# GpSimd's operations on two wide tensors move to VectorE, all but those of the input projection

## The chip, the cores and the metric

The kernel runs on one core of a Trainium2 chip. The metric is device time in microseconds (us), the median of three runs; lower is better. The core has TensorE (PE, matrix multiplication into PSUM), VectorE (DVE), ScalarE (ACT), GpSimd (POOL) and SyncE (SP, which here issues most DMAs). Each engine takes its instructions strictly in the order of its own queue and waits on semaphores for the others. GpSimd does not read PSUM in this kernel.

## The reference

A two-layer decoder trunk on x of 1024 tokens by 1024 channels, in float32. Layer 0 mixes with an HGRN2 recurrence and a Conformer convolution behind one input projection, and one output projection follows. Layer 1 mixes with causal pooling over windows of 2, 4, 8 and 16 tokens. Each layer then attends over 256 memory tokens with four heads and applies a SwiGLU FFN of width 2816. Around each sub-layer: x = LayerNorm(alpha * x + f(x)).

```
y = hybrid_ab_mixer(x, ...)  or  multiscale_pool_mixer(x, ...)
x = layer_norm(ALPHA * x + y, ln_mix_g[l], ln_mix_b[l])
y = memory_cross_attention(x, mem_n, xa_wq[l], xa_wk[l], xa_wv[l], xa_wo[l])
x = layer_norm(ALPHA * x + y, ln_xa_g[l], ln_xa_b[l])
y = swiglu_ffn(x, ffn_wg[l], ffn_wu[l], ffn_wd[l])
x = layer_norm(ALPHA * x + y, ln_ffn_g[l], ln_ffn_b[l])
```

## The kernel before, in words

Every float32 product is made of three matmuls (`mm3`, L208): each operand is split into a high part, a copy rounded to the reduced type by ScalarE, and a low part, the difference, by VectorE or GpSimd (`split`, L214; for weights `split_next`, L112, where `lo_engine` names the engine of the low part, lines L123 and L125). TensorE multiplies low by high, high by low and high by high, and cannot begin on an operand before its low part is there.

Larger products use seven block products in place of eight (Strassen's scheme in Winograd's form). `seven` (L807) runs them: for each product j of an order such as (1, 2, 5, 6, 3, 7, 4), for each half g of the inner dimension, it calls `hook(j, g)`, makes operands ahead (`look`, three or four in hand), and lets TensorE run 24 matmuls over four token blocks p. When a product is through, `add(j, p, bank)` adds each of its four PSUM banks into the result, on VectorE (`add_res`, L247) or by ScalarE copies. Products 1, 6, 7 and 4 accumulate on the same four banks, so that the additions of one must be done before the next writes; products 5 and 3 share another four, and product 2 has its own. There are eight banks. `combos_A` and `combos_B` (L725 to L765) make the sums and differences of blocks that the scheme wants, in steps 0 to 3, two operations of 128x1024 each; the hooks call them. `operands7` (L795) splits the A side's operand with GpSimd and the B side's with VectorE. A product of this kind appears as the output projection (`mixer0_out`), the attention scores (`attn_scores`) and the attention output (`attn_out`), the last two in both layers; each has 14 operands. `build_A` and `build_VWo` make the B sides by ordinary matmuls ahead of them and already issue the first combinations and operands.

The FFN's gate and up products use the same scheme with VectorE alone. The down product (`ffn_down`, L1337) runs 42 operands whose A sides come ready from DRAM; its hooks apply the gain and shift of the preceding norm to eight tiles of x (`AFFINE`, L52; L1371 and L1372), on VectorE or GpSimd.

There is no scheduler: an engine's queue is the order in which the code issues. So an addition that TensorE waits for stands behind everything that the hooks and the operand making have issued to VectorE before it. GpSimd also does the one-column steps of the norms (`ln_a`, L257 and L258; `ln_n`, L268; `rstd`, L228), scales seven of eight softmax tiles of each layer (L939, one operation with a broadcast; the other tile takes four one-head instructions on VectorE, L942), and makes the weights' low parts wherever `lo_engine` says so: in the input projection, in the output projection and the value projection behind it, in the attention output, and from the down product to the next build.

Of the kernel before, what the change touches and what calls it, by code (L numbers as in the profile page):

```python
# [12 lines left out]
ALU = mybir.AluOpType  # L13
AX = mybir.AxisListType

P = 128
# [7 lines left out]
MEM = 256  # L24
HEADS = 4
# [25 lines left out]

AFFINE = {(1, 2): ((0, "vector"), (4, "gpsimd")), (1, 3): ((1, "vector"),), (1, 4): ((2, "vector"), (5, "gpsimd")),  # L52
          (1, 5): ((3, "vector"),), (5, 1): ((6, "gpsimd"),), (5, 3): ((7, "vector"),)}

# [90 lines left out]
class Kern:  # L145
# [442 lines left out]
    def mixer0_out(self):  # L588
        nc = self.nc
        gb = self.ln_params(self.a["ln_mix_g"][0], self.a["ln_mix_b"][0])  # L590
        x = self.x = [None] * NT
        sts = [self.sm("lst", 5) for _ in range(NT)]
        A, B = self.sides
        take2 = lambda: [self.w.take() for _ in range(2)]
        Y = lambda i, k: [self.Y[i, k, g] for g in range(2)]

        def load(t):
            x[t] = self.page("x", [D])
            nc.sync.dma_start(x[t], self.a["x"][t * P:(t + 1) * P, :])

        def add(j, p, b):
            self.add_block(j, b, x[p], x[p + 4], sts[p], sts[p + 4])
            if j == 3:
                self.ln_a(x[p], sts[p])
            if j == 4:
                self.w.ahead(4 + (p + 1) // 2, 7)
                self.ln_a(x[p + 4], sts[p + 4])
                if p > 1:
                    self.ln_b(x[p + 2], sts[p + 2], gb)

        def hook(j, g):
            if j == 1:
                if g == 0:
                    while self.y_ready[2] < 4:
                        self.pump()
                    A[2] = Y(0, 1)
                load(2 * g)
                load(2 * g + 1)
                B[("12", 3)[g]] = take2()
                if g == 1:  # L620
                    self.combos_B(B, 0, nc.vector)
                    self.combos_B(B, 1, nc.gpsimd)
            if j == 2 and g == 0:
                while self.bg or self.bg2:
                    self.pump()
                A["blocks"] = ((A[1], A[2]), (Y(1, 0), Y(1, 1)))
                for i in range(3):
                    self.combos_A(A, i, nc.vector)
                self.combos_B(B, 2, nc.gpsimd)
            if (j, g) in ((2, 1), (5, 0)):  # L630
                load(4 + 2 * (j == 5))
                load(5 + 2 * (j == 5))
            if j == 6 and g == 0:
                self.combos_B(B, 3, nc.vector)
                self.combos_A(A, 3, nc.gpsimd)
            if j == 7:
                self.ln_b(x[2 * g], sts[2 * g], gb)
                self.ln_b(x[2 * g + 1], sts[2 * g + 1], gb)
            if j in (7, 4):
                self.w.ahead(1 + g + 2 * (j == 4), 6)  # L640

        self.w.lo_engine = ("gpsimd",)
        self.w.split_ahead = 0
        self.seven(ORDER_A, self.made, self.src, 2, 4, lambda j: 4 if j in (3, 7) else 3, add, hook, 0)
        self.w.split_ahead = 2
        self.last = [lambda t=t: self.ln_b(x[t], sts[t], gb) for t in (6, 7)]
# [77 lines left out]

    def combos_A(self, A, step, eng):  # L725

        tt = eng.tensor_tensor
        if step == 0:
# [18 lines left out]

    def combos_B(self, B, step, eng):
        tt = eng.tensor_tensor
        if step == 0:  # L750
# [43 lines left out]

    def operands7(self, order, fa, fb, ng, fast=()):  # L795

        for j in order:
            for g in range(ng):
                r = []
                for f, eng in ((fa, "vector" if (j, g) in fast else "gpsimd"), (fb, "vector")):  # L800
                    src = f(j, g)
                    hi, lo = self.page("dh", list(src.shape[1:]), F32R), self.page("dl", list(src.shape[1:]), F32R)
                    self.split(hi, lo, src, eng)
                    r += [hi, lo]
                yield r
# [76 lines left out]
    def build_A(self):  # L882
# [6 lines left out]
        for dc in range(DC):  # L889
# [20 lines left out]
            if dc == 3:  # L910
                A["blocks"] = self.AT
                self.combos_A(A, 0, nc.gpsimd)
            if dc in (4, 5):
# [3 lines left out]
            if dc == 5:  # L917
                self.combos_A(A, 1, nc.gpsimd)
            if dc == 6:
                self.combos_A(A, 2, nc.gpsimd)  # L920
                self.combos_B(B, 0, nc.vector)
        self.combos_B(B, 1, nc.vector)
        self.combos_B(B, 2, nc.vector)
        self.sides = A, B
        self.AT, self.x = [None, None], None

    def softmax(self, p, pool):

# [8 lines left out]
        nc.vector.reciprocal(rs, sm)  # L937
        if pool:
            nc.gpsimd.tensor_tensor(p, p, rs.unsqueeze(2).broadcast_to([P, HEADS, MEM]), op=ALU.mult)  # L939
            return  # L940
        for h in range(HEADS):
            nc.vector.tensor_scalar(p[:, h, :], p[:, h, :], rs[:, h:h + 1], None, op0=ALU.mult)  # L942

    def softmaxes(self, ts):

        live = []
        todo = [self.softmax(self.Pm[t], t in (1, 2, 3, 4, 5, 6, 7)) for t in ts]
        while todo or live:
# [7 lines left out]
    def attn_scores(self):  # L956
# [18 lines left out]
        def hook(j, g):  # L975
            if j == 6 and g == 0:
                self.combos_B(B, 3, nc.vector)
                self.combos_A(A, 3, nc.gpsimd)
            if j in (7, 4):
# [8 lines left out]
    def build_VWo(self):  # L988
# [43 lines left out]
        self.made.append(next(self.src))  # L1032
        self.combos_B(B, 0, nc.vector)
        f = self.blocks_T(view[4:])
        A["blocks"] = ((A[1], A[2]), (f[:2], f[2:]))
        self.combos_B(B, 1, nc.vector)
        self.sides = A, B

    def attn_out(self, layer):
# [3 lines left out]
        sts = [self.sm("lst", 6) for _ in range(NT)]  # L1043
        self.w.lo_engine = ("gpsimd",)

# [12 lines left out]
        def hook(j, g):  # L1058
            if j == 1:
                if g == 0:  # L1060
                    self.combos_A(A, 0, nc.gpsimd)
                else:
                    self.combos_A(A, 1, nc.vector)
                    self.combos_A(A, 2, nc.gpsimd)
            if j == 2 and g == 0:
                self.combos_B(B, 2, nc.vector)
            if (j, g) in ((2, 1), (5, 0)):
# [3 lines left out]
            if j == 6 and g == 0:  # L1071
                self.combos_B(B, 3, nc.vector)
                self.combos_A(A, 3, nc.gpsimd)
            if j in (7, 4):
# [262 lines left out]
    def ffn_down(self, layer):  # L1337
        nc = self.nc
        self.w.split_ahead = 0
        self.w.lo_engine = ("gpsimd",)  # L1340
        x = self.x = [None] * NT
# [19 lines left out]
        def hook(j, g):  # L1361
# [5 lines left out]
            if j == 1 and g == 0:  # L1367
                gx.extend(self.ln_params(self.a["ln_xa_g"][layer], self.a["ln_xa_b"][layer]))
            for t, eng in AFFINE.get((j, g), ()):
                eng = getattr(nc, eng)  # L1370
                eng.tensor_tensor(x[t], x[t], gx[0], op=ALU.mult)  # L1371
                eng.tensor_tensor(x[t], x[t], gx[1], op=ALU.add)  # L1372
            if j == 4 and g == 0:
# [250 lines left out]
```

## Time and profile before

| | |
|---|---|
| median of 3 runs | 2451.51 us (2450.9 to 2452.84) |
| profiled execution | 2451.65 us, span 2449.9 us |
| granted TensorE clock | 0.976 of full speed |
| busy, share of the span | PE 94%, PEld 78%, DVE 73%, ACT 43%, POOL 27% |

The busy share of PE is the union of pipelined matmuls, so 94% says that the array has work queued, not that it runs at its peak. A wait is listed as engine, line and what ended it. The stages, by the names of PSUM tiles in the trace: input projection and recurrence to 395 us; output projection 395 to 503; value projection of the memory to 535; build of the scores' B side to 559; scores to 650; build of the output's B side to 681; attention output to 767; FFN gate and up to 1209, down to 1428; then the second layer in the same order, with the key and value projections and the pooling mixer from 1428 to 1537.

### The profile page before, as it was taken

To read this page: it belongs to the slowest core of one execution; us is meant where nothing else is said; L and a number is where in the kernel's file an instruction comes from. 1 tells how busy PE (TensorE), PEld (TensorE's weight loads), DVE (VectorE), ACT (ScalarE), POOL (GpSimd) and SP (SyncE) were. 2 spreads that over 40 slices of the span, in tenths; PEclk is the share of its full clock that TensorE was granted. 3 is DMA by queue.
4 is the path that set the end of the run, shared out by engine and by line. 5 is a ranking of instruction groups with operands and counts; after the bars stand their busy time and mean duration, and the time that the engine had idled before them with its cause. 6 is when DMAs were issued, how large, how long until landed. Compare 5 with 4: busy or idle time off the path is not lost. (4 is left out here: it accounts for less than half of the span.)

```text
span 2449.9 us, 29443 instructions
## 1 busy us (share of the span) xinstructions
PE 2312.4 (94%) x11208; PEld 1916.5 (78%) x11208; DVE 1778.0 (73%) x2126; ACT 1044.2 (43%) x1727; POOL 665.9 (27%) x401
## 2 busy tenths in 40 slices
PE   8999997797979999999999989798999999999998
PEld 7777776696868888888878789786788888887886
DVE  6986788868795876766774566978767667676555
ACT  3245555344736544444412234546364444342212
POOL 1332346757483000000110073755610000002001
PEclk9999999899989999999999999999999999999999
DMA  5111124050122234435796642302024353449783
GB/s 185 69 35 35 35 90 160 26 187 28 53 77 87 95 130 163 159 125 184 280 356 230 247 142 102 118 1 103 36 85 158 126 182 130 161 176 392 261 291 117
DMA packets 117341, 344.02 MB, mean 140 GB/s; under 512 B 10832, under 2 KB 11344, under 8 KB 117200
## 3 DMA queue, kind: packets, MB, share of 16 engines
q1 hardware_dynamic: 70560, 244.35, 27.7%
q10 hardware_dynamic: 46640, 97.79, 11.1%
q8 instruction: 89, 1.46, 0.2%
q14 instruction: 52, 0.43, 0.1%
HBM read 239.34 MB, written 102.76 MB: 140 GB/s over the span
## 5 line engine op out<-in xcount | busy, mean ns | idle before, releaser
L210 PE MATMUL P<-xh,op 128*128 128x512 f32 x1120 | 436.2, 389 | 2.1 <-ACT u L1301 2.1
L212 PE MATMUL P<-xh,op 128*128 128x512 f32 x1120 | 435.7, 389 | 0.0
L211 PE MATMUL P<-xl,op 128*128 128x512 f32 x1120 | 435.7, 389 | 0.0
L210 PE MATMUL D<-dh,dl 128*128 128x512 f32 x560 | 226.2, 404 | 58.4 <-DVE x L247 35.4
L1371 POOL TENSOR_TENSOR x<-x,lng 128x1024 f32<-128x1024 f32 x6 | 17.9, 2980 | 867.8 <-DVE s L1179 421.4
L210 PE MATMUL D<-dh,wp 128*128 128x512 f32 x616 | 242.4, 394 | 9.5 <-ACT dh L215 8.3
L210 PEld LDWEIGHTS P<-xh,op 128*128 128x128 f32 x1120 | 210.2, 188 | 47.3 <-ACT u L1301 3.8
L211 PE MATMUL D<-dl,wp 128*128 128x512 f32 x616 | 243.0, 395 | 3.3 <-DVE dl L216 3.3
L1113 DVE TENSOR_TENSOR op<-raw,op 128x512 fp32r<-128x512 f32 x200 | 137.9, 689 | 147.5 <-ACT op L1112 147.5
L212 PEld LDWEIGHTS P<-xh,op 128*128 128x128 f32 x1120 | 210.2, 188 | 44.0
L211 PE MATMUL D<-dl,dh 128*128 128x512 f32 x560 | 224.6, 401 | 21.1 <-DVE dl L216 21.1
L211 PEld LDWEIGHTS P<-xl,op 128*128 128x128 f32 x1120 | 210.2, 188 | 43.3
L212 PE MATMUL D<-dh,wp 128*128 128x512 f32 x616 | 241.8, 393 | 0.0
L212 PE MATMUL D<-dh,dh 128*128 128x512 f32 x560 | 223.4, 399 | 0.0
L125 POOL TENSOR_TENSOR wl<-raw,wh 128x1024 fp32r<-128x1024 f32 x64 | 173.5, 2723 | 164.3 <-ACT wh L123 159.9
L216 DVE TENSOR_TENSOR dl<-wp,dh 128x1024 fp32r<-128x1024 f32 x96 | 127.6, 1336 | 115.9 <-ACT dh L215 72.8
L215 ACT CAST dh<-wp 128x1024 fp32r<-128x1024 f32 x96 | 93.8, 989 | 265.4 <-DVE wp L777 57.3
L365 DVE SCALAR_TENSOR_TENSOR cacc<-sig,par,cacc 128x1023 f32<-128x1023 f32 (+14 forms) x120 | 175.5, 1462 | 2.5
L210 PEld LDWEIGHTS D<-dh,dl 128*128 128x128 f32 x560 | 108.8, 194 | 85.5 <-issue 36.6
L257 POOL TENSOR_SCALAR lst<-lst 128x1 f32<-128x1 f32 x48 | 27.3, 568 | 466.7 <-ACT sq L256 466.3
L216 POOL TENSOR_TENSOR dl<-xf,dh 128x1024 fp32r<-128x1024 f32 x48 | 141.5, 2965 | 39.6 <-ACT dh L215 29.2
L216 DVE TENSOR_TENSOR dl<-B,dh 128x1024 fp32r<-128x1024 f32 x48 | 117.9, 2488 | 40.7 <-ACT dh L215 40.7
(272 smaller groups left out, 5236.6 us busy)
## 6 DMA issues: line engine op xcount, KB each, us to landing
wp<-hD SPq DMA_DIRECT2D x140, 512.0 KB, 5.8
hD<-sh ACTq DMA_DIRECT2D x66, 512.0 KB, 3.8
raw<-in_wg SPq DMA_DIRECT2D x44, 512.0 KB, 4.2
raw<-in_wu SPq DMA_DIRECT2D x44, 512.0 KB, 3.3
hD<-hf ACTq DMA_DIRECT2D x44, 512.0 KB, 3.7
hD<-s ACTq DMA_DIRECT2D x44, 512.0 KB, 4.6
wp<-in_wd SPq DMA_DIRECT2D x40, 512.0 KB, 7.8
xD<-x ACTq DMA_DIRECT2D x32, 512.0 KB, 3.8
```

What stands on the lines that cost most here:

```text
L125: eng.tensor_tensor(lo, raw, hi.bitcast(F32), op=ALU.subtract)
L210: mm(out, ll, rh, start=start, stop=False, skip_group_check=more)
L211: mm(out, lh, rl, start=False, stop=False, skip_group_check=more)
L212: mm(out, lh, rh, start=False, stop=stop, skip_group_check=more)
L215: self.nc.scalar.copy(hi, src)
L216: getattr(self.nc, lo_engine).tensor_tensor(lo, src, hi.bitcast(F32), op=ALU.subtract)
L257: nc.gpsimd.tensor_scalar(st[:, 3:4], st[:, 3:4], 1.0 / D, LN_EPS, op0=ALU.mult, op1=ALU.add)
L365: nc.vector.scalar_tensor_tensor(acc[:, s:], u[:, :S - s], w[:, j:j + 1], acc[:, s:], op0=ALU.mult, op1=ALU.add)
L1113: getattr(nc, lo_engine).tensor_tensor(pg[:, 1], src, pg[:, 0].bitcast(F32), op=ALU.subtract)
L1371: eng.tensor_tensor(x[t], x[t], gx[0], op=ALU.mult)
```

## The change

Every wide operation that GpSimd had after the input projection is issued to VectorE at the same place in the code: the A side's low parts in `operands7`, all `combos_A` and `combos_B`, the low parts of weights where `lo_engine` was GpSimd, the affine steps, and the softmax scaling, which becomes four instructions for each tile. GpSimd keeps the one-column steps and the low weight parts of the input projection. The computed values are the same.

```diff
-AFFINE = {(1, 2): ((0, "vector"), (4, "gpsimd")), (1, 3): ((1, "vector"),), (1, 4): ((2, "vector"), (5, "gpsimd")),
-          (1, 5): ((3, "vector"),), (5, 1): ((6, "gpsimd"),), (5, 3): ((7, "vector"),)}
+AFFINE = {(1, 2): (0, 4), (1, 3): (1,), (1, 4): (2, 5), (1, 5): (3,), (5, 1): (6,), (5, 3): (7,)}
@@ mixer0_out, attn_out, ffn_down @@
-        self.w.lo_engine = ("gpsimd",)
+        self.w.lo_engine = ("vector",)
...
-    def combos_A(self, A, step, eng):
-
-        tt = eng.tensor_tensor
+    def combos_A(self, A, step):
+
+        tt = self.nc.vector.tensor_tensor
...
-    def combos_B(self, B, step, eng):
-        tt = eng.tensor_tensor
+    def combos_B(self, B, step):
+        tt = self.nc.vector.tensor_tensor
...
-    def operands7(self, order, fa, fb, ng, fast=()):
-
+    def operands7(self, order, fa, fb, ng):
...
-                for f, eng in ((fa, "vector" if (j, g) in fast else "gpsimd"), (fb, "vector")):
+                for f in (fa, fb):
...
-                    self.split(hi, lo, src, eng)
+                    self.split(hi, lo, src)
@@ build_A, and the other callers alike @@
-                self.combos_A(A, 0, nc.gpsimd)
+                self.combos_A(A, 0)
@@ softmax @@
-        if pool:
-            nc.gpsimd.tensor_tensor(p, p, rs.unsqueeze(2).broadcast_to([P, HEADS, MEM]), op=ALU.mult)
-            return
         for h in range(HEADS):
             nc.vector.tensor_scalar(p[:, h, :], p[:, h, :], rs[:, h:h + 1], None, op0=ALU.mult)
@@ ffn_down, hook @@
-            for t, eng in AFFINE.get((j, g), ()):
-                eng = getattr(nc, eng)
-                eng.tensor_tensor(x[t], x[t], gx[0], op=ALU.mult)
-                eng.tensor_tensor(x[t], x[t], gx[1], op=ALU.add)
+            for t in AFFINE.get((j, g), ()):
+                for r, op in zip(gx, (ALU.mult, ALU.add)):
+                    nc.vector.tensor_tensor(x[t], x[t], r, op=op)
```

## Rows read from the trace of the kernel before

**Rows 1.** The page's first part: busy us (share of span) and instructions of each engine.
```profile
PE 2312.4 (94%) x11208; PEld 1916.5 (78%) x11208; DVE 1778.0 (73%) x2126; ACT 1044.2 (43%) x1727; POOL 665.9 (27%) x401
```
**Rows 2.** Waits of TensorE: engine, line, releaser, us in total, times, longest.
```profile
PE D L210 <- DVE x L247: 35.4, 6, 14.8
PE D L211 <- DVE dl L216: 24.4, 7, 10.6
PE D L210 <- POOL dl L216: 23.0, 5, 9.6
...
PE pa L210 <- POOL wl L125: 1.7, 1, 1.7
```
**Rows 3.** Timeline of TensorE: start, us, instruction, [idle before <- what ended it].
```profile
432.93 0.77 PE L210 MATMUL D<-dh,dl 128*128 128x512 f32 x1 [14.79 <-DVE x L247]
...
490.76 0.77 PE L210 MATMUL D<-dh,dl 128*128 128x512 f32 x1 [12.53 <-DVE x L247]
...
583.11 0.80 PE L211 MATMUL D<-dl,dh 128*128 128x512 f32 x1 [10.55 <-DVE dl L216]
...
706.98 0.80 PE L210 MATMUL D<-dh,dl 128*128 128x512 f32 x1 [9.59 <-POOL dl L216]
...
718.71 0.47 PE L210 MATMUL D<-dh,dl 128*128 128x512 f32 x1 [3.38 <-DVE x L247]
...
1243.00 0.80 PE L210 MATMUL D<-dh,wp 128*128 128x512 f32 x1 [4.14 <-ACT dh L215]
...
1440.79 0.58 PE L210 MATMUL pk<-wh,wl 128*128 128x256 f32 x1 [5.67 <-POOL wl L125]
```
**Rows 4.** Windows: length, busy us and instructions by engine, granted clock, DMA share, GB/s.
```profile
394.70:503.50 108.80, 80.62 (x340) 65.30 (x339) 92.40 (x85) 40.32 (x53) 78.97 (x37) 0.87 0.18 65
...
650.00:680.80 30.80, 29.32 (x160) 24.55 (x159) 26.25 (x32) 27.49 (x66) 15.64 (x8) 1.00 0.41 152
...
767.30:1208.80 441.50, 440.41 (x1973) 364.66 (x1972) 312.28 (x448) 206.07 (x327) 7.98 (x14) 1.00 0.43 152
```
**Rows 5.** Timelines of GpSimd and VectorE: wide operations beside each other and alone.
```profile
479.06 9.88 POOL L125 TENSOR_TENSOR wl<-raw,wh 128x1024 fp32r<-128x1024 f32 x3
...
468.25 1.28 DVE L262 SCALAR_TENSOR_TENSOR x<-x,lst,lng 128x1024 f32<-128x1024 f32 x1
...
476.78 3.39 DVE L262 SCALAR_TENSOR_TENSOR x<-x,lst,lng 128x1024 f32<-128x1024 f32 x1
...
581.84 3.48 DVE L216 TENSOR_TENSOR dl<-B,dh 128x1024 fp32r<-128x1024 f32 x3
```
**Rows 6.** Timeline of VectorE ahead of the first stall of the output projection.
```profile
407.62 2.47 DVE L247 SCALAR_TENSOR_TENSOR x<-x,D 128x512 f32<-128x512 f32 x4
410.01 6.72 DVE L732 TENSOR_TENSOR S<-y,y 128x1024 f32<-128x1024 f32 x2
...
432.10 0.68 DVE L247 SCALAR_TENSOR_TENSOR x<-x,D 128x512 f32<-128x512 f32 x1
```
**Rows 7.** Timeline of VectorE in the build ahead of the scores.
```profile
549.40 0.69 DVE L905 COPY B<-pa 128x512 f32<-128x512 f32 x1 [1.05 <-PE pa L212]
```
**Rows 8.** Timeline of VectorE around the start of the attention output.
```profile
659.53 1.22 DVE L125 TENSOR_TENSOR wl<-raw,wh 128x1024 fp32r<-128x1024 f32 x1
...
688.02 2.47 DVE L865 COPY xf<-xt 128x512 f32<-128x512 f32 x4
...
717.88 0.67 DVE L247 SCALAR_TENSOR_TENSOR x<-x,D 128x512 f32<-128x512 f32 x1
```
**Rows 9.** Groups by line and form: softmax scaling on VectorE; busy us, mean ns, idle before.
```profile
L942 DVE TENSOR_SCALAR p<-p,rs 128x256 f32<-128x256 f32 x8 | 2.3, 349 | 0.1
```
**Rows 10.** Timeline of VectorE in the down product.
```profile
1240.13 1.41 DVE L777 TENSOR_TENSOR wp<-wp,wp 128x1024 f32<-128x1024 f32 x1 [4.36 <-DMA wp<-in_wd]
...
1248.89 1.23 DVE L216 TENSOR_TENSOR dl<-wp,dh 128x1024 fp32r<-128x1024 f32 x1 [1.16 <-ACT dh L215]
```
**Rows 11.** The page's costliest groups: ScalarE's high parts.
```profile
L215 ACT CAST dh<-wp 128x1024 fp32r<-128x1024 f32 x96 | 93.8, 989 | 265.4 <-DVE wp L777 57.3
```

More of the change, by code (lines that the diff above doesn't have):

```diff
@@ L620, in hook @@
                 if g == 1:
-                    self.combos_B(B, 0, nc.vector)
-                    self.combos_B(B, 1, nc.gpsimd)
+                    self.combos_B(B, 0)
+                    self.combos_B(B, 1)
             if j == 2 and g == 0:
@@ L627, in hook @@
                 for i in range(3):
-                    self.combos_A(A, i, nc.vector)
-                self.combos_B(B, 2, nc.gpsimd)
+                    self.combos_A(A, i)
+                self.combos_B(B, 2)
             if (j, g) in ((2, 1), (5, 0)):
@@ L633, in hook @@
             if j == 6 and g == 0:
-                self.combos_B(B, 3, nc.vector)
-                self.combos_A(A, 3, nc.gpsimd)
+                self.combos_B(B, 3)
+                self.combos_A(A, 3)
             if j == 7:
@@ L917, in build_A, with softmax @@
             if dc == 5:
-                self.combos_A(A, 1, nc.gpsimd)
+                self.combos_A(A, 1)
             if dc == 6:
[L920 to L923, printed above, removed]
+                self.combos_A(A, 2)
+                self.combos_B(B, 0)
+        self.combos_B(B, 1)
+        self.combos_B(B, 2)
         self.sides = A, B
         self.AT, self.x = [None, None], None
-    def softmax(self, p, pool):
+    def softmax(self, p):
         nc = self.nc
@@ L946, in softmaxes @@
         live = []
-        todo = [self.softmax(self.Pm[t], t in (1, 2, 3, 4, 5, 6, 7)) for t in ts]
+        todo = [self.softmax(self.Pm[t]) for t in ts]
         while todo or live:
@@ L976, in hook @@
             if j == 6 and g == 0:
-                self.combos_B(B, 3, nc.vector)
-                self.combos_A(A, 3, nc.gpsimd)
+                self.combos_B(B, 3)
+                self.combos_A(A, 3)
             if j in (7, 4):
@@ L1032, in build_VWo @@
         self.made.append(next(self.src))
-        self.combos_B(B, 0, nc.vector)
+        self.combos_B(B, 0)
         f = self.blocks_T(view[4:])
         A["blocks"] = ((A[1], A[2]), (f[:2], f[2:]))
-        self.combos_B(B, 1, nc.vector)
+        self.combos_B(B, 1)
         self.sides = A, B
@@ L1043, in attn_out @@
         sts = [self.sm("lst", 6) for _ in range(NT)]
-        self.w.lo_engine = ("gpsimd",)
+        self.w.lo_engine = ("vector",)
         def add(j, p, b):
@@ L1060, in hook @@
                 if g == 0:
-                    self.combos_A(A, 0, nc.gpsimd)
+                    self.combos_A(A, 0)
                 else:
-                    self.combos_A(A, 1, nc.vector)
-                    self.combos_A(A, 2, nc.gpsimd)
+                    self.combos_A(A, 1)
+                    self.combos_A(A, 2)
             if j == 2 and g == 0:
-                self.combos_B(B, 2, nc.vector)
+                self.combos_B(B, 2)
             if (j, g) in ((2, 1), (5, 0)):
@@ L1071, in hook @@
             if j == 6 and g == 0:
-                self.combos_B(B, 3, nc.vector)
-                self.combos_A(A, 3, nc.gpsimd)
+                self.combos_B(B, 3)
+                self.combos_A(A, 3)
             if j in (7, 4):
@@ L1339, in ffn_down @@
         self.w.split_ahead = 0
-        self.w.lo_engine = ("gpsimd",)
+        self.w.lo_engine = ("vector",)
         x = self.x = [None] * NT
```

## The prediction

> **What bounds the kernel now.** I read the busy shares first, then the waits of TensorE, the timeline around each of its stalls, the windows by stage, and last the timelines of VectorE and GpSimd inside those stages. The chain that ended last is a handful of steps of the last norm and says nothing of the rest. TensorE is busy 94% of the span [rows 1], so this is a TensorE kernel with about 137 us of holes. The waits say who makes them: in the products that accumulate in banks named D, TensorE waited 35.4 us for VectorE's additions (L247), 24.4 us for VectorE's low parts and 23.0 us for GpSimd's low parts (L216) [rows 2]. They are few and long: 14.79 and 12.53 us in the first output projection, 10.55 us at the start of the first attention scores, 9.59 and 3.38 us in the first attention output, 4.14 us at the head of the down product, 5.67 us behind it [rows 3]. The scores, the attention output and the down product come once more in the second layer with the same stalls to within 1 us. In the gate and up products (767 to 1209 us) TensorE is busy 440.41 of 441.50 us and GpSimd hardly works [rows 4]; nothing of the change is there, nor in the input projection.
>
> Why is VectorE late although its busy share is 73%? The same subtraction of 128x1024 takes 1.21 us when GpSimd is idle (three end to end in 3.48 us, so one every 1.135 us), the norm step L262 1.28 us; with a GpSimd operation on two tensors beside it the same L262 takes 3.39 us, and the GpSimd operations take 9.88 us for three [rows 5]; the two operations of L732 take 6.72 us [rows 6]. Two engines together finish one operation each in about 3.3 us; VectorE alone would finish both in 2.3. So GpSimd's help costs VectorE more than the work it takes over, and VectorE is the engine that TensorE waits for.
>
> **The change part by part.** GpSimd loses every operation on two wide tensors after the input projection: low parts of operands and weights, combinations, softmax scaling, the affine steps of the down product. Each goes into VectorE's queue at the place where the code issues it. No DMA is moved; GpSimd issues none and keeps the one-column steps. A wide operation moved costs 1.135 us [rows 5]; its bounds are that and the 3.4 us beside GpSimd [rows 6]. I take the lower, since nothing wide is left on GpSimd to collide with. The sums go against the profiled execution's 2451.65 us (span 2449.9), which is 0.14 us above the median of 2451.51.
>
> First stall of the output projection. Column j=5 needs the banks of j=2, so it waits for the additions of j=2, which stand in VectorE's queue behind combos_A 0, 1 and 2 and the low parts of operands (5,0) and (5,1). The additions of j=1 end at 410.0, those of j=2 begin at 432.10: 22 us for eight operations, most of them at 3.4 [rows 6]. After: combos_A six, combos_B step 2 two, low parts four, twelve in all: 12 x 1.135 = 13.6 us, so 423.7. Gain 8.4. I leave the starting point alone: ahead of it VectorE takes over four operations (4.5 us) and has about as many long ones that shorten by 2.2 each.
>
> Second stall there. Column j=4 adds into the banks of j=7, whose additions stand behind ln_b of four tiles. From the first L262 at 468.25 [rows 5] the queue will hold eight norm steps (10.4 us, at 1.28 and its pitch), two low weight parts and two low operand parts (4 x 1.135 = 4.5): 14.9 us, so additions at 483.1 and TensorE at 483.9 against 490.76 [rows 3]. The norm steps are paced by TensorE ahead of 468.25, so this adds: gain 6.8.
>
> Scores, twice. From the copy at 549.40 [rows 7] to the low part of operand (2,0), which TensorE awaits, stand in the new queue four copies of 0.6, three low weight parts, six low operand parts, combos_A 1 and 2 and combos_B 0, 1 and 2 (ten): 2.4 + 19 x 1.135 = 24.0 us, so 573.4 against 583.11 [rows 3]. Gain 9.6, twice 19.2; about 4.5 us of the stall stays.
>
> Attention output, twice. From the low weight part at 659.53 [rows 8] to operand (2,1): 22 wide operations (four weight parts, eight operand parts, ten of combinations) 25.0; 14 copies of 0.6 (four took 2.47 [rows 8]) 8.4; four softmax scalings as four short instructions each, 2.3 us for eight [rows 9], so 1.15 each, 4.6; two reductions and small steps 3.1. Sum 41.1: operand (2,1) is there at 700.6, not 706.98. Then the four additions (2.4) and six wide operations (6.8): additions of j=2 at 709.8 against 717.88 [rows 8]. Gain 8.1, twice 16.2; the second of the two stalls stays at 3 to 4 us.
>
> Small ones. The wait of 1.7 us for a low weight part at the start of the second layer's build [rows 2] goes. Of the 5.67 us behind the down product [rows 3] about 1 us goes: the split there starts behind the ScalarE copy as before and is shorter by 1.2.
>
> What it costs. In the down product VectorE gets the affine steps of tiles 4, 5 and 6, two operations each (2.3 us). Those of tile 4 fall ahead of a wait of 4.36 us for a weight's DMA [rows 10] and are hidden. Those of 5 and 6 come where VectorE makes each operand by a subtraction, a wait of 1.16 us for ScalarE's copy [rows 10] and a low part, while TensorE uses one in 24 x 0.224 = 5.4 us [rows 4]; right behind the stall of 4.14 us there is little in hand. The bounds are 0 (the slack covers both) and 4.6 us (it covers none) in each layer; I take 3, towards the upper end because TensorE has just waited there, twice 6. If a load of x were late, VectorE's queue would now wait for it with operands behind; each load is issued at least two operands ahead in the code.
>
> TensorE's clock: the mean granted clock in the output projection is 0.87 of full speed [rows 4], that is, part of the time at 1.2 instead of 2.4 GHz behind the stalls; up to 10 us could come back there. I take none, as stalls of 4 to 8 us stay at the same places.
>
> Sum: 8.4 + 6.8 + 19.2 + 16.2 + 1.7 + 1.0 - 6.0 = 47.3 us. 2451.65 - 47.3 = 2404.
>
> **Rivals.** (1) VectorE has no room where it is fullest. In the value-output build (650 to 680.8 us) it is busy 26.25 of 30.80 us [rows 4], and it takes over five scalings and two low parts, 8.1 us; if what shortens there is in other places, TensorE waits for it in both layers: 16 us, 2420. For it: no slack in that row. Against it: the weights are split one head ahead, so a delay of one or two us is covered, and the operations that stand beside GpSimd's now shorten. The Trainium skill has a rule on that side (Perfetto Trace Analysis, "Optimizing Scalar/DVE Operations"): where VectorE is saturated, giving work to GpSimd may make sense, though it says that the two share a read port and that this might not help. By the rule the time is this rival's, by the rows above my forecast's; no run here shows which holds for this stage.
>
> (2) The stalls go whole, since a queue that is earlier in one stage is earlier in the next: 14.79 + 12.53 + 2 x 10.55 + 2 x (9.59 + 3.38) + 5.67 = 80 us [rows 3], 2372. For it: every one of these waits ends on VectorE or GpSimd. Against it: the sums above leave a queue longer than TensorE's work in front of it.
>
> (3) Slower: VectorE now waits for ScalarE in the queue that holds the additions. Each of the 70 low parts taken from GpSimd (14 operands in five products) follows ScalarE's copy of the high part. If VectorE stands before each as it does in the down product, 1.16 us [rows 10], that is 81 us: 2404 + 81 = 2485. It turns the sign from 0.68 us each. Against it: in the five products ScalarE makes the copies of several operands in a row, 93.8 us for 96 [rows 11], 0.98 each, while VectorE takes 1.135 for its part, so ScalarE stays ahead once it is.
>
> That the change does not do what it says can hardly be: the engine is named in each call.
>
> **Chances.** My forecast (2392 to 2416) 0.60; rival 1 or another loss of that size (2416 to 2435) 0.20; rival 2 and its neighbours (2370 to 2392) 0.12; rival 3 0.05; next to nothing either way 0.03. A measurement of this kernel tells about 0.2%, 5 us, from no change; so faster 0.92, same 0.03, slower 0.05. The range of 8 in 10 is 2384 to 2430: it takes in most of rival 1, half of rival 2, and the bounds of the affine steps.
>
> **What would show it.** After the change, low parts and combinations at 1.2 us with no long ones left after the input projection, and VectorE's total not above the 1778 us of [rows 1]. In the output projection stalls of about 8 and 6 us; in the scores one of about 4.5; in the attention output two of 3 to 4. In the down product a stall up to 3 us longer behind the affine steps. The prediction is wrong if wide operations of VectorE stay at 3.4 us, if TensorE's waits for L247 grow, or if VectorE shows new idle time behind ScalarE's copies.

## The result and the profile after

The change takes 2407.95 us (median of 4 runs, 2406.34 to 2408.04) where the kernel before took 2451.48 beside it: ratio 0.982, 95% interval 0.9803 to 0.9837. That is 43.5 us less; the forecast was 47.3 less and 2404. The span went from 2449.9 to 2405.8 us, the mean granted clock from 0.976 to 0.983.

The first part of the page of after (busy us, share of the span, instructions), which answers to [rows 1]:

```profile
PE 2310.7 (96%) x11208; PEld 1914.0 (80%) x11208; DVE 1757.7 (73%) x2336; ACT 1043.4 (43%) x1727; POOL 188.8 (8%) x233
```

VectorE does 210 instructions more and is busy 20 us less. GpSimd has lost 168 instructions and 477 us. TensorE does the same work with fewer holes. The groups by line and form of after (busy us, mean ns, idle before) show why:

```profile
L215 DVE TENSOR_TENSOR dl<-xf,dh 128x1024 fp32r<-128x1024 f32 x48 | 58.5, 1220 | 31.5 <-ACT dh L214 31.5
L215 DVE TENSOR_TENSOR dl<-B,dh 128x1024 fp32r<-128x1024 f32 x48 | 58.5, 1220 | 0.0
L124 DVE TENSOR_TENSOR wl<-raw,wh 128x1024 fp32r<-128x1024 f32 x77 | 92.9, 1220 | 18.7 <-ACT wh L122 18.6
L262 DVE SCALAR_TENSOR_TENSOR x<-x,lst,lnb 128x1024 f32<-128x1024 f32 x31 | 39.8, 1284 | 5.8 <-POOL lst L257 2.9
```

(Line numbers of after are 1 to 6 lower: L246 is the addition that was L247, L215 the low part of L216, L124 the weight's low part of L125. In the other runs they shift by a few lines with the edits.) The first row is the work taken from GpSimd. The other three were 2488, 1963 and 1793 ns in the mean before and are now all at the length they have alone. The idle time in front of the two low parts is 31.5 us in all; before it was 40.7, in front of dl<-B.

TensorE's waits after (engine, line, releaser, us in total, times, longest), which answer to [rows 2]:

```profile
PE D L209 <- DVE x L246: 22.6, 4, 7.8
PE D L209 <- DVE dl L215: 9.4, 2, 4.7
...
PE pk L209 <- DVE wl L124: 6.4, 1, 6.4
PE D L210 <- DVE dl L215: 5.8, 14, 1.5
...
PE xt L271 <- ACT B L1015: 3.2, 2, 1.6
PE xt L271 <- DVE B L1013: 3.1, 2, 1.5
...
PE xt L271 <- DVE kl L215: 2.3, 1, 2.3
```

The waits for GpSimd's low parts (23.0 us) are gone, and those for additions and for VectorE's low parts fell from 59.8 to 37.8. The wait for kl (the low part of a projected memory block) behind the output projection is new. Those for L1015 and L1013 in the value-output build grew; before they were

```profile
PE xt L272 <- ACT B L1020: 2.1, 2, 1.1
PE xt L272 <- DVE B L1018: 0.7, 2, 0.3
```

The stall that was the first of [rows 3] and VectorE's queue ahead of it, which answers to [rows 6], in the timeline of after:

```profile
408.43 2.36 DVE L731 TENSOR_TENSOR S<-y,y 128x1024 f32<-128x1024 f32 x2
...
415.24 2.35 DVE L760 TENSOR_TENSOR wp<-wp,wp 128x1024 f32<-128x1024 f32 x2
...
422.05 0.68 DVE L246 SCALAR_TENSOR_TENSOR x<-x,D 128x512 f32<-128x512 f32 x1
```

```profile
422.89 0.77 PE L209 MATMUL D<-dh,dl 128*128 128x512 f32 x1 [7.80 <-DVE x L246]
```

Twelve wide operations take 13.6 us (408.43 to 422.05), where eight took 22, and TensorE's row behind them has 7.80 us for 14.79.

Windows of after for two rows of [rows 4] (length, busy us and instructions of PE, PEld, DVE, ACT, POOL, granted clock, DMA share, GB/s): the output projection and the first value-output build.

```profile
393.10:488.40 95.30, 81.43 (x340) 66.42 (x339) 83.60 (x108) 40.08 (x53) 6.99 (x13) 0.91 0.22 74
628.00:662.00 34.00, 30.80 (x161) 25.74 (x159) 29.66 (x55) 27.59 (x66) 0.00 (x0) 0.95 0.37 133
```

The first is 13.5 us shorter with more of VectorE's work in it, and the clock is 0.91 in place of 0.87. The second is 3.2 us longer: VectorE went from 26.25 to 29.66 us there.

This table splits the span at the first and last matmul of each product (us). The last five columns are runs told of below; "FFN" is everything from an attention output to the down product, the last 36 matmuls of the attention output included.

| stage | before | after | ops_only | rest_only | back3 | late | best2 |
|---|---|---|---|---|---|---|---|
| ahead of the output projection | 394.7 | 393.1 | 393.0 | 393.4 | 393.4 | 393.7 | 394.0 |
| output projection | 108.8 | 95.3 | 102.3 | 100.9 | 95.5 | 85.1 | 82.2 |
| memory values, score build | 56.0 | 55.5 | 57.0 | 61.1 | 56.4 | 60.1 | 61.6 |
| scores 1 | 90.4 | 84.1 | 80.0 | 86.3 | 82.5 | 76.3 | 76.3 |
| value-output build 1 | 30.9 | 34.0 | 31.0 | 34.1 | 30.7 | 32.4 | 30.8 |
| attention output 1 | 86.4 | 76.8 | 79.4 | 85.0 | 77.5 | 75.1 | 70.4 |
| FFN 1 | 441.5 | 441.4 | 441.4 | 441.4 | 441.4 | 441.7 | 442.0 |
| down product 1 | 219.6 | 221.5 | 219.3 | 221.8 | 219.6 | 221.6 | 220.1 |
| second mixer, memory, build | 139.1 | 134.8 | 143.7 | 138.0 | 142.0 | 134.8 | 134.2 |
| scores 2 | 91.5 | 84.4 | 77.6 | 88.8 | 78.5 | 76.3 | 76.4 |
| value-output build 2 | 30.9 | 32.4 | 30.7 | 32.5 | 30.7 | 35.1 | 30.8 |
| attention output 2 | 87.4 | 78.3 | 79.4 | 86.8 | 77.5 | 75.3 | 72.0 |
| FFN 2 | 441.4 | 441.5 | 441.7 | 441.4 | 441.4 | 441.4 | 441.4 |
| down product 2 | 221.3 | 221.3 | 220.1 | 221.7 | 219.5 | 220.8 | 218.8 |
| tail | 9.8 | 11.3 | 11.3 | 11.3 | 11.3 | 11.6 | 11.4 |

### The profile page after: what moved, and what is told of

The parts are those of the page before. It is cut to its first block, busy times and chain, and to the rows that moved or that the text cites. A ratio compares the mean times of both kernels' runs of the same rounds, so it can differ in the third digit from the quotient of the medians.

```text
span 2405.8 us, 29264 instructions
## 1 busy us (share of the span) xinstructions
PE 2310.7 (96%) x11208; PEld 1914.0 (80%) x11208; DVE 1757.7 (73%) x2336; ACT 1043.4 (43%) x1727; POOL 188.8 (8%) x233
## 3 DMA queue, kind: packets, MB, share of 16 engines
q10 hardware_dynamic: 46640, 97.79, 11.3%
## 5 line engine op out<-in xcount | busy, mean ns | idle before, releaser
L209 PEld LDWEIGHTS P<-xh,op 128*128 128x128 f32 x1120 | 210.2, 188 | 47.3 <-ACT u L1296 3.8
L215 DVE TENSOR_TENSOR dl<-wp,dh 128x1024 fp32r<-128x1024 f32 x96 | 109.8, 1146 | 119.6 <-ACT dh L214 79.3
L209 PEld LDWEIGHTS D<-dh,dl 128*128 128x128 f32 x560 | 108.8, 194 | 60.6 <-issue 27.4
L210 PEld LDWEIGHTS D<-dl,wp 128*128 128x128 f32 x616 | 116.8, 190 | 34.7 <-DVE dl L215 10.5
L209 PEld LDWEIGHTS D<-dh,wp 128*128 128x128 f32 x616 | 117.0, 190 | 34.4 <-ACT dh L214 8.2
L1296 ACT COPY u<-P 128x512 f32<-128x512 f32 x120 | 70.6, 588 | 162.1 <-PE P L211 162.1
L211 PEld LDWEIGHTS D<-dh,wp 128*128 128x128 f32 x616 | 116.8, 190 | 23.9
```

Source lines behind the costliest of these rows:

```text
L209: mm(out, ll, rh, start=start, stop=False, skip_group_check=more)
L210: mm(out, lh, rl, start=False, stop=False, skip_group_check=more)
L211: mm(out, lh, rh, start=False, stop=stop, skip_group_check=more)
L215: getattr(self.nc, lo_engine).tensor_tensor(lo, src, hi.bitcast(F32), op=ALU.subtract)
L1296: nc.scalar.copy(u[j], b)
```

## The experiments

Each is compared with a kernel before that ran beside it (2451.3 to 2451.5 us); ratios are to that. The diffs are shortened: lines are joined or left out, and comments say to which run or place they belong.

**Is it the collision?** Three kernels add to after, beside each low part of an A operand, work on GpSimd that nobody needs.

```diff
+        nc.gpsimd.tensor_scalar(self.tick, hi[:, 0, 0:1].bitcast(F32), 1.0, 0.0, op0=ALU.mult, op1=ALU.add)
+        nc.gpsimd.tensor_tensor(scr, kc, kc, op=ALU.add)                                # read2
+        nc.gpsimd.tensor_scalar(scr, kc, 1.0, 0.0, op0=ALU.mult, op1=ALU.add)           # read1
+        for i in range(2): nc.gpsimd.memset(self.scr, 0.0)                              # write
```

> The kernel after, and beside each low part of an A operand (70 of them) GpSimd gets an operation that nobody needs: once the operand's high part is there (a one-column read of it) it adds two 128x1024 views of a constant and writes a scratch tile. VectorE's list of work is that of the kernel after. Theory (a wide two-input operation on GpSimd and one on VectorE exclude each other): VectorE's low parts next to it are again 2.4 to 3.4 us in place of 1.22, the stalls of the products come back and grow, 2435 to 2490 us. Rival (the gain came from which engine's queue the work stands in): operations stay at 1.22 us, 2405 to 2415 us.

> As the run with the added two-input operation, but GpSimd's added operation reads one 128x1024 view of the constant (a scaling) and writes the scratch tile. If what excludes is any reading of SBUF by GpSimd: VectorE's low parts are lengthened as with two inputs, 2425 to 2490 us. If only two-input operations on GpSimd exclude: 1.22 us, and 2405 to 2415 us.

> As the run with the added two-input operation, but in its place GpSimd fills the scratch tile twice (128x1024 each), reading nothing but the one column. Theory: VectorE's operations stay at 1.22 us, and the time at 2405 to 2415 us. If any wide work on GpSimd holds VectorE up, or if it is the one-column steps of the norms queued behind it on GpSimd that count: 2420 us or more.

Measured: read2 2466.67 us (ratio 1.0061, 1.0045 to 1.0078), read1 2430.77 (0.9912, 0.9897 to 0.9927), write 2408.98 (0.9823, 0.9809 to 0.9838). The same VectorE work with two-input reads beside it is slower than the kernel before; with fills beside it nothing is lost. One input that GpSimd reads is enough to lengthen VectorE's low parts, as the first of read1's two expectations has it. Groups by line and form of read2, GpSimd's added operation and VectorE's low part:

```profile
L801 POOL TENSOR_TENSOR scr<-kc 128x1024 bf16<-128x1024 f32 x70 | 179.5, 2565 | 0.0
L215 DVE TENSOR_TENSOR dl<-xf,dh 128x1024 fp32r<-128x1024 f32 x48 | 96.6, 2012 | 25.1 <-ACT dh L214 25.0
```

The same of read1:

```profile
L801 POOL TENSOR_SCALAR scr<-kc 128x1024 bf16<-128x1024 f32 x70 | 119.1, 1701 | 0.0
L215 DVE TENSOR_TENSOR dl<-xf,dh 128x1024 fp32r<-128x1024 f32 x48 | 74.0, 1541 | 28.6 <-ACT dh L214 28.5
```

The same of write:

```profile
L802 POOL MEMSET scr<- 128x1024 bf16 x140 | 133.0, 950 | 4.0
L215 DVE TENSOR_TENSOR dl<-xf,dh 128x1024 fp32r<-128x1024 f32 x48 | 58.4, 1216 | 31.5 <-ACT dh L214 31.5
```

Operations beside each other, and GpSimd's alone, in the timelines of read2 (start, length):

```profile
390.38 1.22 DVE L215 TENSOR_TENSOR dl<-y,dh 128x1024 fp32r<-128x1024 f32 x1
390.47 2.88 POOL L801 TENSOR_TENSOR scr<-kc 128x1024 bf16<-128x1024 f32 x1
391.51 2.92 DVE L215 TENSOR_TENSOR dl<-wp,dh 128x1024 fp32r<-128x1024 f32 x1
...
584.62 1.90 POOL L801 TENSOR_TENSOR scr<-kc 128x1024 bf16<-128x1024 f32 x1
```

Unhindered they take 1.90 and 1.22, beside each other 2.88 and 2.92. GpSimd's operation starts just behind VectorE's first and ends 1.8 us after that one has given way (391.51 to 393.35); VectorE's second ends 1.1 us after GpSimd's (393.35 to 394.43). They do not share, they take turns. GpSimd's subtraction takes 2.38 alone (at 168.8 us of after), and the pairs of the kernel before 3.3 to 3.4 [rows 5]: again nearly the sum of 2.38 and 1.135. The Trainium skill says this as a rule (SBUF — State Buffer, "Who interferes with whom"): a VectorE instruction with two inputs in SBUF and a GpSimd instruction that reads SBUF exclude each other for the whole instruction, and one that only writes does not contend. All three runs agree with it. The section gives no price for such a pair; here it is 1.7 us on VectorE for a two-input GpSimd operation beside it (2.92 less 1.22).

**Which part of the change brought it?** ops_only moves only the 70 low parts of A operands in the kernel before; rest_only is the complement, after with those 70 back on GpSimd.

```diff
-    for f, eng in ((fa, "vector" if (j, g) in fast else "gpsimd"), (fb, "vector")):   # ops_only, on before
+    for f, eng in ((fa, "vector"), (fb, "vector")):
-    self.split(hi, lo, src)                                                           # rest_only, on after
+    self.split(hi, lo, src, "gpsimd" if f is fa else "vector")
```

> The kernel before with one part of the change: the low parts of the A operands (70) move to VectorE, the rest (combinations, low parts of weights, softmax scaling, affine steps) stays where it was. Theory: the gain goes with the collisions that are left, so a part of the 43.5 us, 15 to 30: 2421 to 2437 us; the operations beside the remaining GpSimd work are still 3.3 us, so the stall at the start of the scores (combinations on GpSimd) is cut less than to 4.7. Rival (one queue or short low parts alone bring it): nearly all, 2408 to 2415 us.

> The kernel after with the low parts of the A operands (70) back on GpSimd; combinations, weights, softmax scaling and affine steps stay on VectorE. It is the complement of the run that moved only those low parts (2409.9 us). Theory as now held (what counts is the collision at the operands, one VectorE low part against one GpSimd low part): 2440 to 2452 us, low parts at 3.3 us again, stalls of 9 to 15 us in the output projection and at the scores. Rival (each operation moved brings its share of the 43.5 us, 98 of 168 wide ones): 2420 to 2432 us.

Measured: ops_only 2409.85 us (0.9828, 0.9814 to 0.9843), rest_only 2446.47 (0.9983, 0.9973 to 0.9992), inside the range of its theory. My first expectation missed, and ops_only came where its rival stood: 70 of the 168 moved operations bring 41.6 of the 43.5 us. The table shows that the other 98 are not idle but cancel. Against ops_only, after gains 7.0 us in the output projection, 1.5 in the score build, 8.9 in the second mixer and build, 2.6 and 1.1 in the attention outputs (21.1), and loses 4.1 and 6.8 in the scores, 3.0 and 1.7 in the value-output builds, 2.2 and 1.2 in the down products (19.0). So the theory that every operation taken from GpSimd is a gain is wrong.

**Which moves were a loss?** back3 is after with three parts on GpSimd again; lo_pool is after with the weights' low parts of three stages there.

```diff
-    self.combos_A(A, k)                      # in the score build, k = 0, 1, 2
+    self.combos_A(A, k, nc.gpsimd)
+    if pool: nc.gpsimd.tensor_tensor(p, p, rs.unsqueeze(2).broadcast_to([P, HEADS, MEM]), op=ALU.mult)
-    nc.vector.tensor_tensor(x[t], x[t], r, op=op)
+    (nc.gpsimd if t in (4, 5, 6) else nc.vector).tensor_tensor(x[t], x[t], r, op=op)
```
```diff
-    self.w.lo_engine = ("vector",)           # lo_pool: mixer0_out, attn_out, ffn_down
+    self.w.lo_engine = ("gpsimd",)
```

> The kernel after with three parts back on GpSimd, in stages that do not overlap: the A combinations made during the score build, seven of the eight softmax scalings, the affine steps of tiles 4 to 6. Theory of rival 1 of the prediction (VectorE has no room there, these moves were a cost): score stages 84.1 and 84.4 us to about 80 and 78 as in the run with only the operands moved, against 1 to 3 us more in the build ahead of each; value-output builds 34.0 and 32.4 to 30.9; down products 221.3 to 219.5 and unchanged; together 2395 to 2402 us. If a collision costs more than the work it takes over in these places too: 2408 to 2416 us.

> The kernel after with the low parts of weights in the output projection, the attention output and behind the down product back on GpSimd. The collisions there are with norm steps. Theory (a pair of operations costs 3.3 us where VectorE alone would finish both in 2.4): the second stall of the output projection 6 to 9 us, the wait behind the down product 5.7 in place of 6.4, together 2408 to 2414 us. Rival (VectorE's queue is what is short there): the second stall 3 to 4 us, 2402 to 2406 us.

back3: 2399.84 us (0.9788, 0.9774 to 0.9803), 8.1 faster than after. The value-output builds went to 30.7 each (34.0 and 32.4) and the down products to 219.6 and 219.5 (221.5 and 221.3): 8.7 us. The combinations, of which I expected several us, gave nothing: scores 1.6 and 5.9 shorter, the builds ahead of them 0.9 and 7.2 longer, where weights' low parts beside them took 2.0 to 3.5 us. The timelines of back3 show why softmax scaling is the exception (GpSimd first, then VectorE beside it):

```profile
630.67 1.89 POOL L937 TENSOR_TENSOR p<-p,rs 128x1024 f32<-128x1024 f32 x1 [2.64 <-DVE rs L935]
640.22 1.89 POOL L937 TENSOR_TENSOR p<-p,rs 128x1024 f32<-128x1024 f32 x1 [7.65 <-ACT xf L863]
```
```profile
630.51 1.19 DVE L929 TENSOR_REDUCE mx<-p 128x4 f32<-128x1024 f32 x1
...
640.48 2.47 DVE L863 COPY xf<-xt 128x512 f32<-128x512 f32 x4
...
651.84 2.91 DVE L215 TENSOR_TENSOR dl<-B,dh 128x1024 fp32r<-128x1024 f32 x1
```

Beside the scaling the reduction takes 1.19 and the copies 0.6 each, as they do without it; only four low parts in each layer are longer beside it (1.8 to 2.9). Most of VectorE's instructions there have one input, so GpSimd's work is free, while on VectorE it holds the copies that free TensorE's banks: in after (VectorE, then TensorE)

```profile
639.19 1.21 DVE L929 TENSOR_REDUCE mx<-p 128x4 f32<-128x1024 f32 x1
...
640.72 1.14 DVE L937 TENSOR_SCALAR p<-p,rs 128x256 f32<-128x256 f32 x4
641.77 0.69 DVE L1013 COPY B<-pv 128x512 f32<-128x512 f32 x1
```
```profile
642.52 0.66 PE L271 MATMUL xt<-kc,p 128*128 128x128 f32 x4 [1.53 <-DVE B L1013]
```

lo_pool: 2415.19 us (0.9844, 0.9828 to 0.9861), 7.2 slower than after and beyond either expectation. Its second stall of the output projection is 12.16 us, nearly all of the 12.53 of [rows 3]; I had allowed 6 to 9. The wait behind the down product is 5.67, as expected. GpSimd's four low parts of weights and what VectorE does beside them, in its timelines:

```profile
463.65 13.15 POOL L124 TENSOR_TENSOR wl<-raw,wh 128x1024 fp32r<-128x1024 f32 x4
```
```profile
464.58 3.44 DVE L215 TENSOR_TENSOR dl<-y,dh 128x1024 fp32r<-128x1024 f32 x1
467.94 3.38 DVE L215 TENSOR_TENSOR dl<-wp,dh 128x1024 fp32r<-128x1024 f32 x1
471.25 3.35 DVE L261 SCALAR_TENSOR_TENSOR x<-x,lst,lng 128x1024 f32<-128x1024 f32 x1
474.71 3.17 DVE L262 SCALAR_TENSOR_TENSOR x<-x,lst,lnb 128x1024 f32<-128x1024 f32 x1
```

Four operations on each side in 13 us; the additions stand behind them. So the weights' low parts on GpSimd are enough to bring back nearly all of that stall (before, a fifth pair stood among these, with an operand's low part on GpSimd).

**Are the stalls that are left the queue's order?** late is after with the combinations issued when an operand needs them; late_before is the same order on the engines of before.

```diff
-    for i in range(3): self.combos_A(A, i)      # at j=2
-    self.combos_B(B, 2)
+    self.combos_A(A, 0)                         # at j=2; at (5,0): A 1, A 2; at (5,1): B 2
-    if j == 7: self.ln_b(x[2 * g], sts[2 * g], gb); self.ln_b(x[2 * g + 1], sts[2 * g + 1], gb)
+    if j == 7 and g == 0: self.ln_b(x[0], sts[0], gb); self.ln_b(x[1], sts[1], gb)
+    if j == 4: self.ln_b(x[2 + g], sts[2 + g], gb)
+    if j == 5: self.late(A, B, g)               # scores, attention output: A 1, A 2, B 1 at g=0, B 2 at g=1
```

> The kernel after, all on VectorE, but the combinations are issued only as early as the operand that needs them: A steps 1 and 2, B step 2 (and in the attention B step 1) at column j=5, two columns later than before or more; the norm's last steps of tiles 2 and 3 in the output projection move from j=7 to j=4. No work is added or removed. Theory (the stalls that are left are queue: VectorE operations ahead of the additions and operands which nobody needs yet): 7.80, 6.07, twice 4.68 and 4.4 us of stall go to 0 to 1.5 each, some 28 us, 2375 to 2388 us. Rival (VectorE is short of time in the whole stage, so the queue only moves): new stalls at j=6 and j=3 of the same sum, 2400 to 2410 us.

> The kernel before, its operations on the engines that they had there, with the late order of the combinations and of the two norm steps alone. Theory (order and collision are two causes): part of the stalls goes, but the operands' low parts are still 3.3 us on both engines: 2415 to 2435 us, low parts of the B side near 2.4 us in the mean as before. Rival (the queue's order was the whole loss, and with it the engine does not matter): 2380 to 2395 us, near the same order all on VectorE.

Measured: late 2383.14 us (0.9717, 0.9703 to 0.9732), late_before 2433.40 (0.9925, 0.9909 to 0.9942). In late the scores are 76.3 us in both layers without a stall over 1.3 us, the first stall of the output projection is down to 1.15 us, the second 3.83. The order is worth 18.1 us on the engines of before and 24.8 on those of after, so the two causes are separate; in the other direction the change of engines is worth 43.5 us in the old order and 50.3 in the late one. B's low parts in late_before average 2375 ns (2488 in before): the order leaves the collisions.

**The versions that follow.** best1 is late with the softmax scalings and the affine steps of tiles 4 to 6 on GpSimd; best2 moves norm steps and stores further back as well; best3 was to split two weights earlier.

```diff
-    if n in (2, 4, 6): self.spill((n - 2, n - 1))              # best2, memory projection
-    if n in (10, 16): self.last.pop(0)()
+    if n in (4, 7, 10, 15): self.last.pop(0)()                 # tiles 2, 3, 6, 7; 0 and 1 at j=4
+    if n in SPILL: self.spill((SPILL[n],))                     # one tile each
-    if j == 7:
-        self.ln_n(x[2 * g], sts[2 * g]); self.ln_n(x[2 * g + 1], sts[2 * g + 1])
+    if j == 7 and g:
+        for t in range(4): self.ln_n(x[t], sts[t])
```
```diff
+    if j == 2 and g == 1 and layer < DEPTH - 1: self.w.ahead(2, 4)     # best3, ffn_down
```

> The kernel with the late combinations (2383.1 us), and seven softmax scalings and the affine steps of tiles 4 to 6 on GpSimd again. From the run with three parts back: value-output builds 30.7 each (here 32.4 and 35.1), down products 219.6 and 219.5 (here 221.6 and 220.8): 9.4 us less, 2371 to 2377 us. The scaling collides with hardly anything, as VectorE's copies out of banks and its reductions beside it keep their 0.68 and 1.20 us. Rival (it collides with the low parts that fill VectorE there, and the loss goes into the attention output): 2378 to 2384 us.

> As the run before it, and three more moves in the order: the last norm steps of tiles 0 and 1 of the output projection go from j=7 to j=4 and those of tiles 2 and 3 into the memory projection; the stores of x on ScalarE's queue there go out one at a time; the four norms on ScalarE in the attention output go behind the copies of its last operand. Theory (the stalls that are left are queue ahead of a needed step): 3.83 at 461 us, 2.89 and 1.80 at 488 us, and twice 3.11 in the attention output go, 10 to 14 us: 2358 to 2366 us. Rival (the norm steps are late where they land): 2368 us or more.

> As the run before it, and the first two weights behind the first down product are split at g=1 of its last column, not in its additions. Theory: the wait of 6.4 us for a low weight part behind the down product goes to 0 to 1, 5 to 7 us less than the run before. If those weights' data come only then, or the split stands in front of operands: 0 to 3 us less or slower.

best1: 2372.25 us (0.9675, 0.9661 to 0.9690), 10.9 less than late, with value-output builds at 30.8 and down products at 219.7 and 220.0 as expected. best2: 2363.24 (0.9638, 0.9624 to 0.9653). That is 9.0 less than best1, short of the 10 to 14 expected. The two waits of 3.11 in the attention output are gone (70.4 and 72.0 us), but in the memory projection they only changed their name. TensorE's timeline of best2 there:

```profile
487.52 0.33 PE L274 MATMUL xt<-kc,x 128*128 128x128 f32 x1 [3.57 <-DVE x L265]
490.36 1.97 PE L274 MATMUL xt<-kc,x 128*128 128x128 f32 x8 [2.52 <-DVE x L265]
```

They were 2.89 and 1.80 on kl in late; now they are longer and wait for the norm steps that I moved there, needed at once by the transposes: the rival in that place. best3: 2364.09 (0.9643, 0.9628 to 0.9657), no gain, and the wait behind the down product stayed at 6.42 us. The edit did not move what it was to move. The first splits behind the down product stand in VectorE's timelines of best2 and of best3 at the same place, 10.8 us ahead of the down product's end (1377.4 and 1375.1), and none stands earlier:

```profile
1366.53 2.36 DVE L127 TENSOR_TENSOR wl<-raw,wh 128x1024 fp32r<-128x1024 f32 x2 [2.31 <-ACT wh L125]
```
```profile
1364.25 2.36 DVE L127 TENSOR_TENSOR wl<-raw,wh 128x1024 fp32r<-128x1024 f32 x2 [2.32 <-ACT wh L125]
```

In the code, `ahead(2, 4)` counts from the next weight to be taken; at that point this is one of the down product's own, which needs no split. So best3 says nothing on this wait.

## Why the prediction came out, term by term

**The reason holds.** "GpSimd's help costs VectorE more than the work it takes over" was read from one pair of rows [rows 5]. read2 and write show it by themselves, and most of the signs named came: low parts and combinations at 1.2 us with no VectorE operation over 1.3 us left, VectorE's total below 1778 us, stalls of 7.80 and 6.07 us (forecast 8 and 6), 4.68 (4.5), 4.35 and 4.42 (3 to 4; the other stall of each attention output nearly went). The stall at the head of the down product did not grow (3.78 and 3.62 us, 4.14 and 4.13 before). That 7.80 and 4.68 fit is partly luck: the prediction's own gains leave 6.4 of the 14.79 us and 1.0 of the 10.55.

**Output projection**: forecast 15.2, measured 13.5. Both queues took what the sums said: 13.62 us for the twelve operations (13.6), and 14.90 from the first norm step (459.57) to the additions (474.47), for 14.9. The first stall ends 8.5 us earlier in its stage (8.4), the second a further 5.4 (6.8): the norm steps begin only 7.1 us earlier, so that the two gains add but for 1.4.

**Scores**: forecast 19.2, measured 6.3 and 7.1 of the stages (13.4). The queue again took what the sum said: in after the copy that answers to the one at 549.40, VectorE's fifth of the build, is at 536.57, and that copy, three more and the 19 wide operations take 24.0 us. The step that failed is the queue's start, which the sum left where it was. Counted from the end of the output projection the copy comes 2.2 us later (48.2 for 45.9): half because TensorE's product is later, half because VectorE now has combos_A 0 ahead of the copy. VectorE's timeline of after:

```profile
533.17 2.35 DVE L731 TENSOR_TENSOR S<-xf,xf 128x1024 f32<-128x1024 f32 x2
...
536.57 0.69 DVE L903 COPY B<-pa 128x512 f32<-128x512 f32 x1
```

Another 1.5 us in the first layer goes with the clock: from the awaited operand to the end of the stage TensorE is busy all but 0.3 us, 66.85 us at a granted clock of 0.98 before, 68.34 at 0.96 after.

**Attention output with the build ahead of it**: forecast 16.2, measured 18.7 in the two products less 4.6 given back in the two builds. The queue took 41.6 us to operand (2,1) and 50.8 to the additions, for 41.1 and 50.3. The first stall of 9.6 us, of which about 3 was to stay, shrank to 0.57: TensorE comes to it later by what it loses in the build.

**Rival 1**, VectorE without room in the value-output build, was true in kind and small in size: 3.1 and 1.5 us, not 8 each. back3 prices it at 3.3 and 1.7. About half of the first is the clock: granted 0.95 over the 34.0 us shown above, so 1.7 us, for a part at 1.2 instead of 2.4 GHz right behind the two longer waits; the second layer's build had 1.00 and is 1.6 us shorter. Which layer it falls in changes: in write the first build has 1.00 (32.4 us) and the second 0.95 (34.0). The Trainium skill's remark that handing work to GpSimd may help a full VectorE, which stood on this side (Perfetto Trace Analysis, "Optimizing Scalar/DVE Operations"), holds in this stage and fails in the products: what decides is the form of VectorE's instructions beside it.

**Affine steps**: forecast a cost of 6; the down products are 1.9 and 0.0 us longer, and back3 prices the steps at 1.9 and 1.8. The 0.0 of the second layer is the clock's: in the last 32 us of that product the granted clock is 0.95 before and 1.00 after, 1.6 us. So the steps cost about 1.8 us a layer, not 3: the slack covered more than I allowed.

**Behind the down product**: forecast a gain of 1.0, measured a wait longer by 0.74 (5.67 to 6.41). The split there does start behind ScalarE's copy, and from the copy's start to TensorE it is 1.2 us shorter, as forecast (3.51 to 2.34). What the sum left out is that the copy itself is later. ScalarE's timelines of before and of after, then VectorE's of after:

```profile
1437.28 1.03 ACT L123 CAST wh<-raw 128x1024 fp32r<-128x1024 f32 x1
```
```profile
1410.40 1.15 ACT L255 ACTIVATE sq<-x,lst 128x1024 bf16<-128x1024 f32 x1 [4.27 <-DVE lst L254]
...
1411.55 1.03 ACT L122 CAST wh<-raw 128x1024 fp32r<-128x1024 f32 x1
```
```profile
1398.99 2.36 DVE L124 TENSOR_TENSOR wl<-raw,wh 128x1024 fp32r<-128x1024 f32 x2 [2.31 <-ACT wh L122]
...
1412.61 1.23 DVE L124 TENSOR_TENSOR wl<-raw,wh 128x1024 fp32r<-128x1024 f32 x1 [2.30 <-ACT wh L122]
```

The copy stands on ScalarE behind a norm's square, which waits for VectorE's additions and norm steps, and these now stand behind two low parts of weights and a wait for ScalarE. So it starts 9.8 us behind the down product's last matmul, not 8.9; of the forecast 1.2 us 0.2 is left, and TensorE comes to the wait 1.0 sooner. The wait of 1.7 us in the second layer's build went as forecast, and that stage as a whole is 4.3 shorter against the 2.7 of both terms.

**Rival 2** (the stalls go whole) fell as argued, and late shows that what kept them was order. **Rival 3** fell: VectorE's idle time behind ScalarE's copies did not grow at the operands (31.5 against 40.7 us). It did in front of weights' low parts (5.1 to 18.6), as just told. So 47.3 against 44.1 us of span is partly luck: the scores (5.8 too high), the build (4.6 not in the sum), the output projection (1.7) and a tail longer by 1.5 stand against the affine steps (4.1 too dear), the attention outputs (2.5) and 1.6 each in the second mixer and ahead of the output projection. There nothing was changed, and the runs differ by more (392.2 to 394.7 us).

What stays open: the mean clock's part in the gain was not measured by itself, the memory projection's waits in best2 and the one behind the down product were not removed, and the longer tail was not looked into.

## What to carry to other kernels

Before work is given to GpSimd, look at what VectorE does at that moment: beside instructions with one input the help was nearly free here, beside those with two it cost most of GpSimd's operation (1.7 of 1.90 us). A queue counted instruction by instruction, from the code as well as from the trace, came out to within about half a us in all four queues counted. Where it starts is a second question: moved work also stands ahead of the last thing done, and that was this prediction's largest error. When a stall's queue holds work that nobody needs yet, moving that work later brings much too (24.8 us here, beside 43.5 for the change of engines), and the two add. And look in the trace whether an edit moved what it was to move.

## What the runs showed that was not expected

GpSimd can wait through a whole row of VectorE's operations. In write, where GpSimd's one-column read has 0.19 us of work, it took 11.29; the timelines (GpSimd, then VectorE):

```profile
410.66 11.29 POOL L798 TENSOR_SCALAR tick<-dh 128x1 f32<-128x1 f32 x1 [8.51 <-ACT dh L214]
421.89 1.96 POOL L802 MEMSET scr<- 128x1024 bf16 x2
```
```profile
410.46 2.35 DVE L738 TENSOR_TENSOR y<-y,y 128x1024 f32<-128x1024 f32 x2
...
420.69 1.21 DVE L215 TENSOR_TENSOR dl<-wp,dh 128x1024 fp32r<-128x1024 f32 x1
421.82 0.68 DVE L246 SCALAR_TENSOR_TENSOR x<-x,D 128x512 f32<-128x512 f32 x1
```

It ends when VectorE turns from operations with two SBUF inputs to the additions out of banks, ten operations later. At other places GpSimd waited for one operation (1.16 us) and the engines took turns; what decides between the two was not found. The norms' own one-column steps, which stay on GpSimd, took up to 1.6 us in after and not more, and VectorE's second norm step (L262) waited 2.9 us in all for them (4.3 before), so here this cost little; in a kernel that keeps VectorE on two-input work for long it could hold a norm.
